# Moving an adaptive-modulation weight stream towards the gate projections, and the sums of h into the first up-projection group

## The chip, the cores and the metric

The kernel runs on one core of a Trainium2 chip. The metric is the device time of one execution in microseconds (us). The engines named below are PE (TensorE, the matrix engine), DVE (VectorE), ACT (ScalarE), POOL (GpSimd) and SP (SyncE, which here only issues DMAs). Each works through its own queue in order. A tile of 128 partitions by 512 columns of float32 is 256 KB.

## What is computed

One layer of a hybrid decoder on 512 tokens of width 2048, in float32. A vector c gives six modulation rows; two mixers and a feed-forward part with a causal convolution of width 3 follow:

```python
mod = (silu(c) @ w_ada + b_ada)[:, None, :]
sh_a, sc_a, gt_a, sh_f, sc_f, gt_f = jnp.split(mod, 6, axis=-1)
h = rms_norm(x, g_attn) * (1.0 + sc_a) + sh_a
# h @ w_in gives, among others, the columns gate_a and gate_b (2048 each)
merged = sigmoid(gate_a) * (o_a @ w_pa) + sigmoid(gate_b) * (o_b @ w_pb)
x = x + gt_a * (merged @ w_o)
h = rms_norm(x, g_ffn) * (1.0 + sc_f) + sh_f
u = conv3_causal(h @ w_up)
x = x + gt_f * ((silu(u[..., :5632]) * u[..., 5632:]) @ w_down)
```

Here o_a is a sparse attention (8 heads, keys chosen by an indexer) and o_b a dense latent attention (8 heads).

## The kernel before, in words

**Arithmetic.** Each float32 operand is split into a rounded part hi and a rest lo (`split`: ACT makes hi, L116, DVE makes lo, L117), and a product is three matmuls, hi x hi, hi x lo and lo x hi (`mm3`, L120 to L122). Weights pass through `wtile`: SP loads a pair of 128-row blocks, 512 KB, into a raw tile (L105), ACT and DVE split it (L109, L110) into one of three hi/lo pairs. These instructions get a high priority.

**Order.** The framework arranges the instructions of each engine at build time, from a simulated timeline, with the place in the program as priority. A later part can so fill the gaps of an earlier one, but the order on the chip is fixed. Data dependences go by the program: who writes a tile waits for all who used it before in the program.

**Storage.** There are 75 slots of 128 x 512 (`get` takes the one that has been free longest, `put` gives it back), eight PSUM banks, and five raw tiles, used strictly in turn by the weights and by the ada stream (`raw_tile`). In the middle of the kernel banks 0 to 3 (`MM`) serve projections; banks 4 to 7 (`AT`) serve the attention and are handed out in turn by `at_bank()`.

**Stages**, with their place in the profiled span: the first four modulation rows' part and the indexer's projections (to 230 us), the indexer and the query projection (to 350), attention A interleaved with the gate projections (to 550), the rest of the gates (to 667), the latent projections MKV and MQ (`C_MKV`, `C_MQ`), attention B interleaved with the projection by w_pa, the projection by w_pb (to about 1160), the output projection by w_o (to 1355), the second norm that makes h2, up group 0 (to 1455), then 40 pairs of column blocks of the up projection by a scheme of seven products in place of eight (L1258 to L1260), and the down projection.

The gate projections are eight blocks (`gate_block`). Blocks 0 to 5 stand right after attention A in the program, block 6 after the latent projections. A block calls `lin_fm`, which runs over the 16 row blocks two at a time: 8 ticks of 24 matmuls (block 7 has 2 ticks). `pa_block` and the loop over w_pb have 4 ticks for each of four column blocks; the output projection has 8 ticks for each of four. After each tick a function `tick` may be called.

**The ada stream.** 16 column blocks of w_ada are not needed until later (gt_a, sc_f, sh_f, gt_f). `ada_stream` is a generator: each call of `next` loads 512 KB into a raw tile (L715) and adds it on DVE to an accumulator (two operations, L720 for the first of a block and L722). Eight calls make a block; the ninth puts the finished block on the list `pend` and begins the next. There are two accumulators, used alternately. `ticker(rate)` adds `rate` to a credit at each tick and calls `next` for every whole unit: TG holds the rates of the gate blocks, TP that of w_pa, TB of w_pb, TO of w_o. What is left over runs after w_o.

`flush_cols(b)` finishes the blocks of `pend`: it splits the accumulator into two new slots, sums over the partitions with two matmuls into bank b (L749, L750), and then either loads b_ada into the accumulator by a DMA on POOL, adds the bank (L754) and stores the result to DRAM (L755, eight of the blocks), or picks the diagonal into `mod` (L758 and the lines behind it). Before, it is called at the start of each block of the gates, of w_pa, w_pb and w_o, with the fourth bank of those that the block will use.

**The sums of h.** The seven-product scheme needs four sums of quarters of h2, `tsum`. They are formed from `x1T`, 16 tiles that hold the normed and scaled x: four steps, each with 8 DVE operations on half tiles (L1123 to L1126) and 4 splits. They stand behind up group 0 in the program. `up_group(0)` runs `lin_fm` twice (gate and value columns, 16 ticks in all), with the convolution (`conv`) at the end of each.

Of the kernel before, what the change touches and what calls it, by code (L numbers as in the profile page):

```python
# [14 lines left out]
AF = mybir.ActivationFunctionType  # L15
ALU = mybir.AluOpType
AX = mybir.AxisListType

P = 128
T = 512  # L20
D = 2048
KD = D // P
# [4 lines left out]
C_MQ, C_MKV, C_GA, C_GB = 2640, 3152, 3472, 5520  # L27
# [4 lines left out]
def trunk_layer_kernel(  # L32
# [9 lines left out]
    U1=4,  # L42
    U2=10,
    PLAN="A0 A1|A2 A3|B0 B1 B2 B3|A4 A5 A6 A7|B4 B5 B6 B7|A8 A9 A10 A11|B8 B9 B10 B11|A12 A13 A14 A15 B12 B13 B14 B15",
    TG=(0, 1, 1, 1, 1, 1, 1, 1),
    TP=1.5,
    TB=1.5,
    TO=1,
    HG=2,
    AFT=(-1,),  # L50
    PEU=((2, 5, 8, 11, 14),) * 2 + ((),) * 6,
# [2 lines left out]
    V, A, G, PE, SP = nc.vector, nc.scalar, nc.gpsimd, nc.tensor, nc.sync  # L54
# [18 lines left out]
    def getr():  # L73
        return get(F32R)

    def put(*ts):
        for t in ts:
            free.append(held.pop(id(t)))
# [45 lines left out]
    def lin_fm(src, c0, act, K, banks, evac, tick=None, M=4):  # L124
        kn = 8 // M
        for kg in range(0, K, kn):
            wh, wl = wtile(src, kg, kn, c0, M * P)
            for m in range(M):
                ms = slice(m * P, (m + 1) * P)
                for i in range(kn):  # L130
                    k = kg + i
                    ah, al = act[k]
                    mm3(banks[m], wh[:, i, ms], wl[:, i, ms], ah, al, k == 0, k == K - 1)
                if kg + kn == K:
                    evac(m, banks[m])
            if tick:
                tick()
# [16 lines left out]
    def half():  # L154
        cnt["half"] += 1
        return bank[4:8] if cnt["half"] % 2 == 0 else bank[0:4]
# [94 lines left out]
    for ks in (range(0, 7), range(7, 14), range(14, KD)):  # L251
# [4 lines left out]
        for k in ks:  # L256
            t = get()
# [16 lines left out]
    h = []  # L274
# [95 lines left out]
    for g in range(-2, 8):  # L370
# [7 lines left out]
        if 0 <= g + 1 < 8:  # L378
            ada_cols(g + 1)
            for k in (2 * g + 2, 2 * g + 3):  # L380
                hi, lo, t = getr(), getr(), ht[k % 2]
# [108 lines left out]
    MM = bank[0:4]  # L490
# [10 lines left out]
    b = bank[7]  # L501
# [10 lines left out]
    b = bank[6]  # L512
# [7 lines left out]
    for tb in range(1, 4):  # L520
        S = (tb + 1) * P
        qiT = []
        for cb in range(2):
            t = qi[tb, cb]
            rope(t.rearrange("p (h d) -> p h d", d=64), 8, 16, "i", tb)
            b = at_bank()
# [8 lines left out]
        for hd in range(16):  # L535
            ps = slice((hd % 2) * 64, (hd % 2) * 64 + 64)
            q = (hd % 8) // 2
            b = at_bank()
# [20 lines left out]
        gt, eq, pre = rl[1][:, :S], rl[2][:, :S], wk[:, :S]  # L559
# [30 lines left out]
    for tb in range(4):  # L590
        t = kva[tb]
# [8 lines left out]
    for g in range(2):  # L600
        b = at_bank()
# [105 lines left out]
    ada_acc = [get(), get()]  # L707
# [20 lines left out]
    pend = []  # L728
# [2 lines left out]

    credit = [0.0]

    def ticker(rate):
        def tick():
            credit[0] += rate
            while credit[0] >= 1.0:
                credit[0] -= 1.0
                next(stream, None)
        return tick  # L740

# [2 lines left out]
    def flush_cols(b):  # L744
        while pend:
            cb, acc = pend.pop(0)
            hi, lo = getr(), getr()
            split(hi, lo, acc)
            PE.matmul(b, ones_r, hi, start=True, stop=False)  # L749
            PE.matmul(b, ones_r, lo, start=False, stop=True)  # L750
            put(hi, lo)
            if cb in gtr_d:
                G.dma_start(acc, b_ada[0:1, cb * 512:(cb + 1) * 512].to_broadcast([P, T]))
                V.tensor_tensor(acc, acc, b, ALU.add)  # L754
                G.dma_start(gtr_d[cb], acc)  # L755
            else:
                a3 = acc.rearrange("p (q n) -> p q n", q=4)
                V.tensor_tensor(a3, b.rearrange("p (q n) -> p q n", q=4),  # L758
                                ident[:, None, :].to_broadcast([P, 4, P]), ALU.mult)
                s4 = sm.tile([P, 4], F32, name="ss4")  # L760
                V.tensor_reduce(s4, a3, axis=AX.X, op=ALU.add)
                mod_cols(mod[:, cb * 4:cb * 4 + 4], s4, col1[:, cb * 4:cb * 4 + 4])
# [11 lines left out]
    gate_d = [dram.tile([P, T], F32, name=f"gate{k}") for k in range(2 * KD)]  # L774
# [4 lines left out]
    def ev_store(dst, j0):  # L779
        def ev(m, b):  # L780
            t = gst[m % 2]
            if m % 2:
                V.tensor_copy(t, b)
            else:
                A.activation(t, b, AF.Copy)
            G.dma_start(dst[j0 + m], t)
        return ev

    def gate_block(n):
        flush_cols(MM[3])  # L790
        j0 = 3 + n * 4
        lin_fm(w_in, C_GA + j0 * P, h, KD, MM, ev_store(gate_d, j0), tick=ticker(TG[n]), M=1 if n == 7 else 4)

    for n in range(GA1):
        gate_block(n)
# [148 lines left out]
    def pa_block(cb):  # L944
        flush_cols(MM[3])
        lin_fm(w_pa, cb * 512, oa, 8, MM, ev_store(pa_d, cb * 4), tick=ticker(TP))

# [54 lines left out]
    for cb in range(4):  # L1002
        bk = half()
        flush_cols(bk[3])
        lin_fm(w_pb, cb * 512, ob, 8, bk, ev_pb(load_gates(cb)), tick=ticker(TB))
    for t in ob:
# [37 lines left out]
    for db in range(4):  # L1044
        bk = half()
# [13 lines left out]
    bk = half()  # L1059
# [5 lines left out]
    h2 = []  # L1065
    lo_i = []
    for k in range(KD):
        t = x1T[k]
# [10 lines left out]
    def conv(j, b):  # L1079
        t = get()  # L1080
        A.activation(t, b, AF.Identity, bias=wcv[:, 3, j:j + 1], scale=wcv[:, 2, j:j + 1])
        V.scalar_tensor_tensor(t[:, 1:], b[:, :T - 1], wcv[:, 1, j:j + 1], t[:, 1:], op0=ALU.mult, op1=ALU.add)
        V.scalar_tensor_tensor(t[:, 2:], b[:, :T - 2], wcv[:, 0, j:j + 1], t[:, 2:], op0=ALU.mult, op1=ALU.add)
        return t
# [2 lines left out]
    NG = DFF // 512  # L1087
    f_d = [dram.tile([P, T], F32, name=f"f{j}") for j in range(NF_)]

    def up_group(grp):  # L1090
        gt = []

        def ev_g(m, b):
            t = conv(grp * 4 + m, b)
            A.activation(t, t, AF.Silu)
            gt.append(t)

        bk = half()
        flush_cols(bk[3])
        lin_fm(w_up, grp * 512, h2, KD, bk, ev_g)  # L1100

        def ev_v(m, b):
            t = conv(44 + grp * 4 + m, b)
            V.tensor_tensor(t, t, gt[m], ALU.mult)
            G.dma_start(f_d[grp * 4 + m], t)
            put(t, gt[m])

        lin_fm(w_up, 512 + grp * 512, h2, KD, half(), ev_v)

    up_group(0)  # L1110
    put(*ada_acc)


    HT = T // 2
    KH = KD // 2
    tsum = [[], [], [], []]
    for i in range(KH // 2):
        raw = [get() for _ in range(4)]
        for j in range(2):
            k, o = 2 * i + j, slice(j * HT, (j + 1) * HT)  # L1120
            ta, tb_ = x1T[k], x1T[k + KH]
            b1, b2 = mod[:, 48 + k:49 + k], mod[:, 48 + k + KH:49 + k + KH]
            V.tensor_tensor(raw[0][:, o], ta[:, HT:], ta[:, :HT], ALU.subtract)  # L1123
            V.scalar_tensor_tensor(raw[1][:, o], tb_[:, HT:], b2, raw[0][:, o], op0=ALU.add, op1=ALU.subtract)
            V.scalar_tensor_tensor(raw[2][:, o], ta[:, :HT], b1, raw[1][:, o], op0=ALU.add, op1=ALU.subtract)
            V.scalar_tensor_tensor(raw[3][:, o], tb_[:, :HT], b2, raw[1][:, o], op0=ALU.add, op1=ALU.subtract)  # L1126
            put(ta, tb_)
        for n in range(4):
            hi, lo = getr(), getr()
            split(hi, lo, raw[n])  # L1130
            tsum[n].append((hi, lo))
        put(*raw)

    def quarter(k0, c0):
        return [(h2[k0 + k][0][:, c0:c0 + HT], h2[k0 + k][1][:, c0:c0 + HT]) for k in range(KH)]
# [131 lines left out]
    for j in range(NF_):  # L1267
        t = get()
# [63 lines left out]
```

## Time and profile before

| | us |
|---|---|
| median of 3 runs | 2770.88 |
| lowest, highest | 2768.09, 2776.09 |
| the profiled execution | 2772.84 |
| its span | 2771.1 |

Page lines and views are read so. In the groups, a row names the line, engine and operation, the written and the read tiles, the count, the busy time, the mean of one in ns, and then the idle time of the engine before these instructions with what ended it. In a window row stand the start and end, the length, then for PE, PEld (weight loads), DVE, ACT and POOL the busy time with the number of instructions (x), then the granted clock of TensorE as a share, the mean share of the DMA engines and GB/s; where a row is for one line alone, only the engines that it uses are listed. A wait row names who waited for whom, the total, the times and the longest. A timeline row has the start, the duration, engine, line and operation, and in brackets the idle time before it and what ended it.

### The profile page before, as it was taken

How to read it: one execution, taken by the hardware profiler on the slowest of the kernel's cores; microseconds unless marked ns; L12 is line 12 of the kernel's file. 1: busy time of each engine (PE TensorE's matmuls, PEld its weight loads, DVE VectorE, ACT ScalarE, POOL GpSimd, SP SyncE). 2: the span in 40 equal slices, each digit the busy share in tenths (PEclk: the TensorE clock that was granted, in tenths of full speed). 3: DMA queues.
4: the chain of work that ended last, by engine and by line, in shares of the span. 5: the costliest groups of instructions: out<-in, count | busy, mean ns of one | idle time of the engine just before them, and what ended most of it. 6: DMA issues, size and time to landing. Idle time of an engine off the chain costs nothing.

```text
span 2771.1 us, 38675 instructions
## 1 busy us (share of the span) xinstructions
PE 2684.6 (97%) x15040; PEld 2293.4 (83%) x15040; DVE 1858.2 (67%) x2931; ACT 1110.5 (40%) x1637; POOL 225.3 (8%) x443
## 2 busy tenths in 40 slices
PE   6999999999999999998998999999999999999998
PEld 5877777788886767776788999999999997888887
DVE  6987975544467676745658888888888873325333
ACT  4333433322344555222434555555555553223221
POOL 1000010100122232100000000000000030000000
PEclk8999999999999999999999999999999999999999
DMA  9943245565475397765422333333333373243232
GB/s 322 356 141 96 60 138 165 183 215 173 125 233 163 128 314 235 267 201 184 139 84 99 119 121 120 118 123 117 121 118 120 121 276 131 91 129 122 94 104 84
DMA packets 197931, 432.93 MB, mean 156 GB/s; under 512 B 18122, under 2 KB 59492, under 8 KB 197748
## 3 DMA queue, kind: packets, MB, share of 16 engines
q1 hardware_dynamic: 168884, 348.59, 39.2%
q0 software_dynamic: 28832, 81.88, 8.6%
q8 instruction: 117, 1.92, 0.3%
q14 instruction: 66, 0.54, 0.1%
q10 hardware_dynamic: 32, 0.01, 0.0%
HBM read 388.46 MB, written 41.94 MB: 155 GB/s over the span
## 4 chain that ended last, share of the span: by engine, by line
PE 74%; issue 13%; DMA 6%; DVE 4%; POOL 1%; ACT 1%; SPq 0%; POOLq 0%; DVEq 0%; ACTq 0%
PE bank L120 14%; PE bank L121 14%; PE bank L122 14%; PE bank L1259 10%; PE bank L1258 10%; PE bank L1260 10%; DMA raw<-in_w_ada 3%; DMA slot<-in_w_ada 1%; DVE wlo L110 1%; DVE slot L722 1%; PE bank L676 1%; DMA raw<-in_w_in 1%; PE bank L931 1%; DMA slot<-in_x 0%; DMA slot<-gate 0%
## 5 line engine op out<-in xcount | busy, mean ns | idle before, releaser
L109 ACT ACTIVATE whi<-raw 128x1024 fp32r<-128x1024 f32 (+4 forms) x302 | 314.3, 1042 | 828.9 <-PE bank L122 506.2
L1259 PE MATMUL bank<-slot,whi 128*128 128x256 f32 x2240 | 628.5, 281 | 7.0 <-DVE slot L117 7.0
L1258 PE MATMUL bank<-slot,whi 128*128 128x256 f32 x2240 | 628.3, 281 | 5.0 <-ACT slot L116 3.2
L1260 PE MATMUL bank<-slot,wlo 128*128 128x256 f32 x2240 | 624.2, 281 | 0.0
L120 PE MATMUL bank<-whi,slot 128*128 128x512 f32 (+2 forms) x1472 | 575.0, 395 | 24.1 <-DVE slot L754 9.9
L121 PE MATMUL bank<-wlo,slot 128*128 128x512 f32 (+2 forms) x1472 | 579.3, 394 | 4.8 <-DVE wlo L110 4.5
L122 PE MATMUL bank<-whi,slot 128*128 128x512 f32 (+2 forms) x1472 | 566.9, 391 | 0.0
L110 DVE TENSOR_TENSOR wlo<-raw,whi 128x1024 fp32r<-128x1024 f32 (+4 forms) x302 | 362.9, 1203 | 301.2 <-ACT whi L109 298.2
L116 ACT ACTIVATE whi<-raw 128x1024 fp32r<-128x1024 f32 x280 | 297.4, 1062 | 339.9 <-PE bank L1259 248.7
L1258 PEld LDWEIGHTS bank<-slot,whi 128*128 128x128 f32 x2240 | 424.1, 189 | 5.9 <-ACT slot L116 3.5
L1259 PEld LDWEIGHTS bank<-slot,whi 128*128 128x128 f32 x2240 | 422.5, 189 | 7.2 <-DVE slot L117 7.2
L1260 PEld LDWEIGHTS bank<-slot,wlo 128*128 128x128 f32 x2240 | 419.9, 189 | 0.0
L117 DVE TENSOR_TENSOR wlo<-raw,whi 128x1024 fp32r<-128x1024 f32 x280 | 341.7, 1221 | 67.6 <-ACT whi L116 65.3
L120 PE MATMUL bank<-slot,whi 128*128 128x512 f32 (+1 forms) x912 | 361.0, 401 | 3.4 <-ACT slot L1072 1.4
L121 PE MATMUL bank<-slot,whi 128*128 128x512 f32 (+1 forms) x912 | 363.5, 399 | 0.1
L122 PE MATMUL bank<-slot,wlo 128*128 128x512 f32 (+1 forms) x912 | 357.5, 399 | 0.0
L120 PEld LDWEIGHTS bank<-whi,slot 128*128 128x128 f32 x1472 | 280.0, 190 | 91.5 <-DVE slot L754 11.4
L121 PEld LDWEIGHTS bank<-wlo,slot 128*128 128x128 f32 x1472 | 280.4, 190 | 67.5 <-DVE wlo L110 7.7
L122 PEld LDWEIGHTS bank<-whi,slot 128*128 128x128 f32 x1472 | 278.7, 189 | 61.2 <-issue 0.9
L722 DVE SCALAR_TENSOR_TENSOR slot<-raw,c_act,slot 128x512 f32<-128x512 f32 x240 | 179.7, 749 | 126.5 <-DMA raw<-in_w_ada 123.6
L117 DVE TENSOR_TENSOR slot<-slot,slot 128x512 fp32r<-128x512 f32 x136 | 92.2, 692 | 194.6 <-PE bank L121 188.7
L120 PEld LDWEIGHTS bank<-slot,whi 128*128 128x128 f32 (+1 forms) x912 | 170.7, 187 | 43.8 <-ACT whi L109 2.1
(279 smaller groups left out, 2619.9 us busy)
## 6 DMA issues: line engine op xcount, KB each, us to landing
raw<-in_w_ups SPq DMA_DIRECT2D x160, 512.0 KB, 3.5
raw<-in_w_ada SPq DMA_DIRECT2D x128, 512.0 KB, 4.9
raw<-in_w_down SPq DMA_DIRECT2D x88, 512.0 KB, 3.6
raw<-in_w_in SPq DMA_DIRECT2D x82, 512.0 KB, 3.7
slot<-in_w_ada SPq DMA_DIRECT2D x128, 256.0 KB, 6.0
raw<-in_w_o SPq DMA_DIRECT2D x32, 512.0 KB, 4.8
f<-slot POOLq DMA_DIRECT2D x44, 256.0 KB, 2.4
slot<-f POOLq DMA_DIRECT2D x44, 256.0 KB, 6.5
```

The lines of the kernel that those rows point to most:

```text
L109: A.activation(hi, raw[:, :w], AF.Copy)
L110: V.tensor_tensor(lo, raw[:, :w], r32(hi), ALU.subtract)
L116: A.activation(dst_hi, src, AF.Copy)
L117: V.tensor_tensor(dst_lo, src, r32(dst_hi), ALU.subtract)
L120: PE.matmul(o, lh, rh, start=first, stop=False)
L121: PE.matmul(o, lh, rl, start=False, stop=False)
L122: PE.matmul(o, ll, rh, start=False, stop=last)
L676: PE.matmul(ob[:, kc * P:], vf(kc), pt[3 - kc], start=kc == 0, stop=kc == 3)
L722: V.scalar_tensor_tensor(acc, t[:, i], c_act[:, k:k + 1], acc, op0=ALU.mult, op1=ALU.add)
L1258: PE.matmul(o, wh[:, ks], rh, start=first and k == 0, stop=False, skip_group_check=True)
L1259: PE.matmul(o, wh[:, ks], rl, start=False, stop=False, skip_group_check=True)
L1260: PE.matmul(o, wl[:, ks], rh, start=False, stop=last, skip_group_check=True)
```

## The change

The rates of the ada stream change: gate blocks from (0, 1, 1, 1, 1, 1, 1, 1) to (1, 1.5, 1.5, 1.5, 1.5, 1.5, 1.5, 1), w_pa and w_pb from 1.5 to 1, w_o from 1 to 0.5. In the gate blocks `flush_cols` is no longer called at the start with the fourth projection bank; instead `tick` calls it, when a finished block is on `pend`, before the next call of the stream, with a bank from `at_bank()`. The four steps of the sums become a function, called after ticks 2, 4, 6 and 10 of up group 0; each of the raw tiles of a step is put back as soon as it is split, and the two ada accumulators are put back ahead of up group 0 rather than behind it.

```diff
-    TG=(0, 1, 1, 1, 1, 1, 1, 1),
-    TP=1.5,
-    TB=1.5,
-    TO=1,
+    TG=(1, 1.5, 1.5, 1.5, 1.5, 1.5, 1.5, 1),
+    TP=1,
+    TB=1,
+    TO=0.5,
...
-    def ticker(rate):
+    def ticker(rate, fb=None):
         def tick():
             credit[0] += rate
             while credit[0] >= 1.0:
                 credit[0] -= 1.0
+                if fb and pend:
+                    flush_cols(fb())
                 next(stream, None)
         return tick
...
     def gate_block(n):
-        flush_cols(MM[3])
         j0 = 3 + n * 4
-        lin_fm(w_in, C_GA + j0 * P, h, KD, MM, ev_store(gate_d, j0), tick=ticker(TG[n]), M=1 if n == 7 else 4)
+        lin_fm(w_in, C_GA + j0 * P, h, KD, MM, ev_store(gate_d, j0), tick=ticker(TG[n], at_bank), M=1 if n == 7 else 4)
...
-    up_group(0)
-    put(*ada_acc)
...
     tsum = [[], [], [], []]
-    for i in range(KH // 2):
+
+    def sum_step(i):
         raw = [get() for _ in range(4)]
...
             tsum[n].append((hi, lo))
-        put(*raw)
+            put(raw[n])
+
+    steps_done = [0]
+
+    def sum_tick():
+        steps_done[0] += 1
+        if steps_done[0] in (2, 4, 6, 10):
+            sum_step(len(tsum[0]))
+
+    def up_group(grp):
...
-        lin_fm(w_up, grp * 512, h2, KD, bk, ev_g)
+        lin_fm(w_up, grp * 512, h2, KD, bk, ev_g, tick=sum_tick)
...
-        lin_fm(w_up, 512 + grp * 512, h2, KD, half(), ev_v)
+        lin_fm(w_up, 512 + grp * 512, h2, KD, half(), ev_v, tick=sum_tick)
+
+    put(*ada_acc)
+    up_group(0)
```

More of the change, by code (lines that the diff above doesn't have):

```diff
@@ L1088, in trunk_layer_kernel @@
     f_d = [dram.tile([P, T], F32, name=f"f{j}") for j in range(NF_)]
[L1090 to L1099, printed above, removed]
-        lin_fm(w_up, grp * 512, h2, KD, bk, ev_g)
[L1102 to L1106, printed above, removed]
-        lin_fm(w_up, 512 + grp * 512, h2, KD, half(), ev_v)
-    up_group(0)
-    put(*ada_acc)
     HT = T // 2
@@ L1131, in trunk_layer_kernel, with ev_g, ev_v @@
             tsum[n].append((hi, lo))
-        put(*raw)
+            put(raw[n])
[5 more added lines that the diff above has]
+    def up_group(grp):
+        gt = []
+        def ev_g(m, b):
+            t = conv(grp * 4 + m, b)
+            A.activation(t, t, AF.Silu)
+            gt.append(t)
+        bk = half()
+        flush_cols(bk[3])
+        lin_fm(w_up, grp * 512, h2, KD, bk, ev_g, tick=sum_tick)
+        def ev_v(m, b):
+            t = conv(44 + grp * 4 + m, b)
+            V.tensor_tensor(t, t, gt[m], ALU.mult)
+            G.dma_start(f_d[grp * 4 + m], t)
+            put(t, gt[m])
+        lin_fm(w_up, 512 + grp * 512, h2, KD, half(), ev_v, tick=sum_tick)
+    put(*ada_acc)
+    up_group(0)
     def quarter(k0, c0):
```

## The prediction

> **What bounds the kernel now.** I read the busy table of the page first, then the span in windows of 50 and 10 us for stretches where TensorE (PE) loses matmuls, then in those the waits and the timeline.
>
> ```profile
> span 2771.1 us, 38675 instructions
> PE 2684.6 (97%) x15040; PEld 2293.4 (83%) x15040; DVE 1858.2 (67%) x2931; ACT 1110.5 (40%) x1637; POOL 225.3 (8%) x443
> ```
>
> PE has work nearly always, so only stalls of PE can be gained. The busy column hides them; the number of matmuls in a window (x) shows them.
>
> ```profile
> 1150.00:1200.00 50.00, 47.66 (x202) 37.34 (x200) 33.11 (x46) 11.28 (x13) 3.22 (x6) 1.00 0.71 231
> 1200.00:1250.00 50.00, 45.57 (x183) 35.92 (x183) 24.65 (x33) 11.56 (x17) 3.25 (x6) 0.93 0.55 180
> 1250.00:1300.00 50.00, 45.30 (x188) 36.02 (x187) 25.21 (x33) 11.57 (x17) 3.24 (x6) 0.97 0.60 199
> 1300.00:1350.00 50.00, 44.54 (x176) 34.82 (x176) 22.90 (x29) 11.79 (x17) 3.24 (x6) 0.93 0.54 179
> ...
> 2300.00:2350.00 50.00, 50.00 (x217) 40.40 (x216) 17.27 (x18) 14.02 (x18) 0.00 (x0) 1.00 0.29 95
> ```
>
> The last row is a full window: 217 matmuls of 512 columns, 50/217 = 0.230 us each, so one tick (24 matmuls, one pair of weight rows) is 5.53 us. In the output projection (1200 to 1350) 34 + 29 + 41 = 104 matmuls are missing: 24.0 us.
>
> ```profile
> DVE slot L722 <- DMA raw<-in_w_ada: 72.6, 22, 6.2
> ...
> PE bank L120 <- DVE slot L754: 9.9, 3, 4.2
> ...
> PE bank L121 <- DVE wlo L110: 4.5, 3, 2.2
> ```
> ```profile
> 1313.19 0.75 DVE L722 SCALAR_TENSOR_TENSOR slot<-raw,c_act,slot 128x512 f32<-128x512 f32 x1 [2.27 <-DMA raw<-in_w_ada]
> 1313.86 0.68 DVE L1028 TENSOR_TENSOR slot<-slot,slot 128x512 f32<-128x512 f32 x1
> 1314.46 0.68 DVE L754 TENSOR_TENSOR slot<-slot,bank 128x512 f32<-128x512 f32 x1
> 1315.06 0.68 DVE L1028 TENSOR_TENSOR slot<-slot,slot 128x512 f32<-128x512 f32 x1
> 1315.66 1.22 DVE L110 TENSOR_TENSOR wlo<-raw,whi 128x1024 fp32r<-128x1024 f32 x1
> ```
>
> The reason is VectorE's (DVE) order: an ada step (L722) waits there for its DMA, 72.6 us in this stage, and behind it stand the flush that must empty the fourth bank (L754) and the weight split (L110). PE waits for both.
>
> The second loss lies where up group 0 ends and the seven-product scheme begins:
>
> ```profile
> 1450.00:1460.00 10.00, 8.92 (x54) 7.73 (x52) 9.25 (x13) 6.77 (x9) 1.13 (x2) 1.00 0.29 107
> 1460.00:1470.00 10.00, 1.44 (x5) 1.14 (x5) 10.00 (x20) 3.20 (x6) 1.08 (x2) 0.60 0.30 105
> 1470.00:1480.00 10.00, 7.64 (x45) 7.15 (x46) 5.76 (x10) 4.85 (x9) 0.00 (x0) 0.72 0.00 1
> 1480.00:1490.00 10.00, 10.00 (x87) 10.00 (x86) 9.04 (x11) 4.01 (x4) 0.00 (x0) 1.00 0.33 107
> ```
> ```profile
> PE bank L1259 <- DVE slot L117: 7.0, 1, 7.0
> PE bank L1258 <- ACT slot L116: 3.2, 1, 3.2
> ```
> ```profile
> 1402.47 0.89 DVE L1125 SCALAR_TENSOR_TENSOR slot<-slot,mod,slot 128x256 f32<-128x256 f32 x2
> ...
> 1459.02 0.68 DVE L117 TENSOR_TENSOR slot<-slot,slot 128x512 fp32r<-128x512 f32 x1
> ...
> 1469.98 4.31 DVE L117 TENSOR_TENSOR slot<-slot,slot 128x512 fp32r<-128x512 f32 x7
> ```
>
> With 87 as full, 82 + 42 = 124 matmuls of 256 columns are missing, 14.2 us. The sums of h are half done by 1403, then stand until 1459: their next slots are those that the convolution of up group 0 gives back at its end.
>
> **The change part by part.**
>
> *Sums.* Nothing is removed and no DMA is in it; L1123 to L1126 and 16 splits are issued inside up group 0. Asked for earlier, they get slots that are long free: at its start 32 of h2 and 16 of x1T are held of 75, so 27 are free once the two accumulators are put back; step 0 takes 12 and returns 8, as do the others. The work after 1459 (12 of the 16 splits at 0.6 us, and some 5 us of L1123 to L1126, 12 us together) moves before 1450.
>
> ```profile
> 1420.00:1430.00 10.00, 10.00 (x44) 8.06 (x43) 2.45 (x2) 2.12 (x2) 0.00 (x0) 1.00 0.17 54
> 1430.00:1440.00 10.00, 10.00 (x44) 8.09 (x44) 1.76 (x2) 2.12 (x2) 0.00 (x0) 1.00 0.33 105
> ```
>
> DVE has over 15 us idle in these two rows alone, so the work costs nothing there; without that cover it would cost its 12 us. What is late next is the last convolution, already in the 1450 row; I leave 2 us. Gain 14.2 - 2 = 12 us (9 to 14).
>
> *Output projection.* TO falls from 1 to 0.5: 16 ada steps instead of some 30, one per 11 us. Their loop (split L110 frees the raw tile, the DMA lands, L722, the next L110) takes about 0.1 + 5 + 1.4 + 1.2 = 7.7 us, over the 5.53 us of a tick and under two ticks. So the waits go; flushes remain at two block starts, at 2 to 3 us each. Of 24 us, 18 are gained (10 to 22).
>
> *Branch projections.* TP and TB fall from 1.5 to 1. The stall there:
>
> ```profile
> 1030.00:1040.00 10.00, 6.43 (x21) 3.20 (x20) 8.30 (x19) 7.27 (x10) 2.48 (x5) 0.94 1.08 401
> 1040.00:1050.00 10.00, 8.01 (x23) 4.78 (x23) 2.32 (x9) 9.03 (x16) 2.15 (x4) 0.55 0.60 210
> ```
>
> DMA is full in the first row; fewer ada steps leave it room. But attention, ACT and reloads are in it too. I take 4 us with the fewer flushes in the main banks (0 to 8).
>
> *Gates.* TG puts 82 calls of the stream into the gate blocks instead of 50: 8 in block 0, 12 in blocks 1 to 6, 2 in block 7. Each is one DMA and two DVE operations:
>
> ```profile
> L722 DVE SCALAR_TENSOR_TENSOR slot<-raw,c_act,slot 128x512 f32<-128x512 f32 x240 | 179.7, 749 | 126.5 <-DMA raw<-in_w_ada 123.6
> ...
> raw<-in_w_ada SPq DMA_DIRECT2D x128, 512.0 KB, 4.9
> ```
>
> The added wait is in the flush. It now takes an attention bank, and in the program all of attention A stands ahead of it: 137th use, the bank that head 7 used for its second group of transposes. So the first flush (call 10) waits for the end of attention A, and the third ada block (call 17) waits for its accumulator. Behind it stand, on DVE the L722 of all later calls, on SP their DMAs (no raw tile comes free), on POOL the flush's load and store among the gate stores; the order in a queue is fixed when the program is built, so weights whose DMA stands behind such an ada DMA wait too. At rate 1.5 the five tiles are used in two ticks, so the weights keep two tiles of their own and go on, until the latent projections use all five.
>
> ```profile
> 500.00:530.00 30.00, 0.00 (x0) 1.00 0.48 156
> 530.00:560.00 30.00, 11.25 (x15) 1.00 0.75 239
> ...
> 587.00:604.00 17.00, 10.16 (x14) 1.00 0.81 250
> 604.00:633.00 29.00, 1.10 (x2) 1.00 0.58 198
> 633.00:651.00 18.00, 9.76 (x13) 1.00 0.76 246
> ```
> ```profile
> 540.00:550.00 10.00, 0.87 (x5) 0.64 (x5) 1.00 0.86 274
> 550.00:560.00 10.00, 0.00 (x0) 0.00 (x0) 1.00 0.95 309
> ```
> ```profile
> 531.75 0.69 DVE L754 TENSOR_TENSOR slot<-slot,bank 128x512 f32<-128x512 f32 x1 [2.99 <-PE bank L750]
> ...
> 535.45 0.49 DVE L720 TENSOR_SCALAR slot<-raw,c_act 128x512 f32<-128x512 f32 x1 [1.20 <-DMA gtr<-slot]
> ```
> ```profile
> 669.01 0.54 POOL L786 DMA_DIRECT2D gate<-slot  x1 [0.46 <-DVE slot L783]
> ```
>
> The first five rows (L722 alone, two operations a step, the first of a block being L720) show this wait in the kernel before: no step from 500 to 530, then bursts of 8 steps, each held until the next block's flush. The transposes (L668, next rows) end near 548; from L754 to the next L720 are 3.7 us, so call 17 starts near 553. Block 5 ends with its store at 669; the second weight tile of the latent projection needs call 66 some 7 us before its use, by 662. These are 50 calls in 109 us, three of them loaded: 47 x r + 3 x 1.5 us, where r = 2.22 us just fits. The bursts give 17/8 = 2.1 and 18/8 = 2.3 us with three to five tiles loaded beforehand; I take 2.6 without that: 127 us, and PE stands for 127 - 109 = 18 us; 2 less for the flushes that no longer wait for a gate bank: 16 us. Ends, counted likewise: 2 (r = 2.3) and 35 (r = 3). Until 550 the same 16 calls run as before: 0 (-4 to +6).
>
> [...]
>
> [...]
>
> *Sum.* -12 - 18 - 4 + 16 = -18 us on the profiled execution's 2772.8 us: 2754.8. That run lay 2.0 us above the median of 2770.9, so 2753 us.
>
> **The rivals.**
>
> *The stream catches up in time.* If the bursts' 2.1 to 2.3 us hold, the stall is 0 to 4 us, say 2: about 2770.9 - 34 + 2 = 2739. For it: DVE was at 10.2 of 17 us with L722 in a burst and PE lost little there. Against: those bursts began with loaded tiles.
>
> *The gates become the bound (slower).* The stream stands until attention A ends, and its backlog holds the latent projections. If the three ada tiles give only r = 3.75 us, as the weakest row did (530 to 560: 8 steps in 30 us), the stall is 47 x 3.75 + 4.5 - 109 = 72 us, and the time 2770.9 + 72 - 34 = 2809. It decides from a stall of 34 us on, r = 2.94 us. For it: the bursts end after 8 steps, so no row shows a longer run at under 3 us. Against: 250 GB/s in the bursts left room.
>
> *The change doesn't do what it says in the output projection.* If the step that is left still stands ahead of the evacuation at block starts, the 18 us shrink to 5: 2766. For it: three of the stalls are at block starts, and loads and stores of x meet there. Against: half the steps, and a loop shorter than two ticks.
>
> **How the numbers follow.** Forecast 0.50 (2753, itself 2741 to 2767), catch-up in time 0.20 (2739), gates bound 0.17 (2772 to 2809), output projection unmoved 0.13 (2766). The range 2732 to 2778 leaves out the upper part of the third and a tail below. Some 0.3% (8 us) is what a measurement can tell from no change: under 2762.6 is faster, over 2779.2 slower. Faster: 0.20 + 0.46 = 0.66; slower: 0.14, from the third; the rest, 0.20, is the same.
>
> **What would show it.** Right: 87 matmuls in every 10 us window of the 30 us after up group 0; over 205 matmuls in each 50 us window of the output projection; no L722 between call 16 and the end of attention A, then a run of 50 calls with DMA over 300 GB/s; a PE stall near the first latent projection, with SP waiting there for L722. Wrong: the first flush done before head 7's transposes (no backlog), a stall over 34 us, or DVE still waiting over 40 us for ada DMAs in the output projection.

## The result, and the profile after

The changed kernel takes 2732.15 us (median of 4 runs, 2731.34 to 2732.21), the kernel before beside it 2773.49 us (4 runs, 2768.09 to 2778.7): a ratio of 0.985, with 0.9829 to 0.9872 as its 95% interval. Some 41 us were gained where 18 were forecast. The profiled execution took 2732.16 us. First the busy table of its page:

```profile
span 2730.4 us, 38657 instructions
...
PE 2668.3 (98%) x15040; PEld 2284.3 (84%) x15040; DVE 1855.8 (68%) x2931; ACT 1112.2 (41%) x1639; POOL 229.0 (8%) x443
```

As before, the busy column tells little; the windows tell where matmuls are missing. The next fence has the changed kernel's windows, all engines: the output projection, the end of up group 0, and the end of the gates.

```profile
1150.00:1200.00 50.00, 50.00 (x217) 40.42 (x216) 27.27 (x36) 12.34 (x17) 5.93 (x11) 1.00 0.60 199
1200.00:1250.00 50.00, 50.00 (x217) 40.41 (x216) 21.72 (x27) 12.95 (x19) 3.24 (x6) 1.00 0.54 172
1250.00:1300.00 50.00, 50.00 (x217) 40.44 (x216) 21.81 (x26) 12.87 (x18) 2.70 (x5) 1.00 0.55 172
...
1420.00:1430.00 10.00, 10.00 (x49) 8.21 (x48) 8.37 (x11) 4.44 (x6) 0.60 (x1) 1.00 0.18 54
1430.00:1440.00 10.00, 10.00 (x87) 10.00 (x86) 9.40 (x11) 4.68 (x8) 1.62 (x3) 1.00 0.40 147
1440.00:1450.00 10.00, 10.00 (x86) 10.00 (x86) 9.18 (x11) 4.94 (x6) 0.00 (x0) 1.00 0.40 121
...
660.00:670.00 10.00, 4.01 (x18) 3.34 (x18) 8.15 (x14) 0.60 (x1) 1.17 (x3) 0.72 0.82 263
670.00:680.00 10.00, 3.21 (x8) 1.79 (x7) 8.84 (x15) 0.63 (x1) 0.43 (x1) 0.50 0.85 265
680.00:690.00 10.00, 7.34 (x33) 7.34 (x34) 3.60 (x7) 2.21 (x3) 0.00 (x0) 0.59 0.62 184
690.00:700.00 10.00, 10.00 (x70) 10.00 (x69) 2.26 (x3) 1.95 (x3) 0.00 (x0) 1.00 0.47 134
```

The output projection has 217 matmuls in each row, the full number, where it had 202, 183 and 188. The seven-product scheme now starts at full speed: 87 and 86 matmuls in the rows behind 1430, no row of 5. The new loss is in the three rows from 660 to 690, where the latent projections begin. They hold 18 + 8 + 33 = 59 matmuls where three rows like that from 690 hold 210: 151 are missing, 21.6 us. PE was idle for 30 - 14.6 = 15.4 us of them; the rest is matmuls at a granted clock of 0.50 to 0.72.

To put numbers on the stretches I counted in the traces when a certain matmul starts: the 1100th, 1700th, 2300th and 3900th of the 7152 that read a split weight outside the seven-product scheme, and then the first matmul of the second norm, the first and last of the scheme, and the last of all. Their order on PE is the program's, so the times between two of them compare like with like, except that the end of attention A can move between the second and the third stretch. In us:

| stretch | before | after | difference | forecast |
|---|---|---|---|---|
| to the 1100th (gates begin) | 358.1 | 353.4 | -4.7 | 0 |
| to the 1700th (end of attention A) | 186.0 | 179.5 | -6.5 | 0 |
| to the 2300th (gates end, latent projections) | 136.6 | 162.3 | +25.7 | +16 |
| to the 3900th (attention B, w_pa, w_pb) | 469.1 | 456.9 | -12.2 | -4 |
| to the second norm (w_o) | 204.4 | 176.0 | -28.4 | -18 |
| up group 0 | 100.9 | 100.8 | -0.1 | 0 |
| seven-product scheme | 809.8 | 794.5 | -15.3 | -12 |
| the rest | 497.1 | 497.9 | +0.8 | 0 |
| last matmul starts | 2762.0 | 2721.3 | -40.7 | -18 |

The stall went as foretold. The windows of the ada steps' line in the changed kernel (busy time and count of L722 on DVE, then the clock, the DMA share and GB/s):

```profile
400.00:410.00 10.00, 4.49 (x6) 1.00 0.91 296
410.00:420.00 10.00, 0.00 (x0) 1.00 0.57 186
...
530.00:540.00 10.00, 0.00 (x0) 1.00 0.44 140
540.00:550.00 10.00, 1.41 (x2) 1.00 0.25 80
...
560.00:570.00 10.00, 5.24 (x7) 1.00 1.01 353
...
670.00:680.00 10.00, 6.78 (x10) 0.50 0.85 265
```

No step between 410 and 540, then a run without a pause. How fast it is stands in the group of the DMA's line, for 540 to 690 (the count, the issue's ns, the first and last start):

```profile
L715 SPq DMA_DIRECT2D raw<-in_w_ada x49: 367/368/512, 549.3 to 676.1; - x49
```

49 loads from 549.3 to 676.1 are 126.8/48 = 2.64 us a step; the prediction had taken r = 2.6 and a start near 553. A load takes 5.3 us from issue to landing there in the median, so the last one lands near 681; PE resumes at 682.7. Who kept PE waiting from 650 to 700 (total, times, longest):

```profile
PE bank L120 <- ACT whi L109: 6.4, 1, 6.4
PE bank L120 <- DVE slot L785: 6.0, 2, 3.2
PE bank L751 <- ACT slot L116: 2.5, 1, 2.5
```

SP's own waits from 540 to 700 show what holds the loads:

```profile
SPq L715 <- DVE slot L722: 67.6, 48, 6.5
```

Two things stand behind the backlog: the next weights (the split, L109, waits for a raw tile) and the emptying of the last gate block's banks (L785 here is L783 of the kernel before), which DVE does in order behind L722. The forecast named the first only. The stretch to the 2300th matmul grew by 25.7 us, 4 more than the stall: 636 matmuls lie in it against 616.

### The profile page after: what moved, and what is told of

Its sections match the earlier page's. It is cut to its first block, busy times and chain, and to the rows that moved or that the text cites. A ratio compares the mean times of both kernels' runs of the same rounds, so it can differ in the third digit from the quotient of the medians.

```text
span 2730.4 us, 38657 instructions
## 1 busy us (share of the span) xinstructions
PE 2668.3 (98%) x15040; PEld 2284.3 (84%) x15040; DVE 1855.8 (68%) x2931; ACT 1112.2 (41%) x1639; POOL 229.0 (8%) x443
## 4 chain that ended last, share of the span: by engine, by line
PE 88%; issue 5%; DMA 4%; DVE 2%; ACT 1%; POOL 1%; SPq 0%; DVEq 0%; POOLq 0%; ACTq 0%
PE bank L120 18%; PE bank L121 18%; PE bank L122 18%; PE bank L1268 9%; PE bank L1267 9%; PE bank L1269 9%; DMA slot<-in_w_ada 1%; PE bank L676 1%; PE bank L932 1%; PE bank L692 1%; PE bank L668 1%; DMA slot<-gate 0%; DMA slot<-in_x 0%; DMA raw<-in_w_down 0%; PE bank L933 0%
## 5 line engine op out<-in xcount | busy, mean ns | idle before, releaser
L109 ACT ACTIVATE whi<-raw 128x1024 fp32r<-128x1024 f32 (+4 forms) x302 | 314.3, 1042 | 823.5 <-PE bank L122 538.2
L722 DVE SCALAR_TENSOR_TENSOR slot<-raw,c_act,slot 128x512 f32<-128x512 f32 x240 | 179.2, 747 | 112.5 <-DMA raw<-in_w_ada 109.6
L122 PEld LDWEIGHTS bank<-slot,wlo 128*128 128x128 f32 (+1 forms) x912 | 171.3, 188 | 42.3 <-DVE wlo L110 1.9
```

The source lines that it names most:

```text
L109: A.activation(hi, raw[:, :w], AF.Copy)
L122: PE.matmul(o, ll, rh, start=False, stop=last)
L722: V.scalar_tensor_tensor(acc, t[:, i], c_act[:, k:k + 1], acc, op0=ALU.mult, op1=ALU.add)
```

## The experiments

All of these kernels compute the same layer. "Ahead at the end of attention A" means: the start of the last score matmul (L692) compared with the kernel before, plus 0.23 us for each weight matmul done more by then (0.230 us is the full rate), less what the run was ahead at the first matmul of L302. That line sums the first modulation rows, which the first normalised column block waits for; it starts near 34 or 38 us, and the expectations give these times to the column block.

**One half each.** First the sums alone, with the rates, the ticker and the gate blocks of the kernel before; then the stream alone, with the sums behind up group 0.

```diff
-    TG=(1, 1.5, 1.5, 1.5, 1.5, 1.5, 1.5, 1),
-    TP=1,
-    TB=1,
-    TO=0.5,
+    TG=(0, 1, 1, 1, 1, 1, 1, 1),
+    TP=1.5,
+    TB=1.5,
+    TO=1,
...
     def gate_block(n):
+        flush_cols(MM[3])
```

> Only the sums of h are moved; rates and flushes as before. Local theory: the 15 us that PE loses around 1450 to 1480 in the kernel before vanish, nothing else moves: about 2758 us (ratio 0.9945). Rival (the moved sums only crowd DVE in up group 0, the gain of the whole change comes from the stream): 2765 to 2775 us, with new PE losses between 1360 and 1450.

```diff
-        lin_fm(w_up, grp * 512, h2, KD, bk, ev_g, tick=sum_tick)
+        lin_fm(w_up, grp * 512, h2, KD, bk, ev_g)
...
-    put(*ada_acc)
     up_group(0)
+    put(*ada_acc)
...
+    for i in range(KH // 2):
+        raw = [get() for _ in range(4)]
```

> Only the stream is moved; the sums stay behind up group 0. Local theory: the rest of the gain, 41 - 15 = 26 us, so about 2747 us, with the loss of 15 us in the first windows of the seven-product scheme still there and a PE stall of some 22 us at the first latent projection. Rival (the two parts only pay together): under 10 us gained, 2763 us or more.

The sums alone: 2756.73 us, ratio 0.9937 (0.9915 to 0.996). The seven-product stretch took 793.0 us there, 16.8 less, and nothing else moved by over 3 us. The stream alone: 2752.77 us, ratio 0.9919 (0.9899 to 0.9939). The two parts are independent and add up: some 17 to 20 and 21 to 24 us (against 2773.49 and 2776.25, the medians of the kernel before in the two sets of runs).

**The output projection.** w_o back at one step a tick, w_pa and w_pb at 0.5 so that the number of steps fits; then the same with each finished block flushed after a tick, into a bank that the block does not use.

```diff
-    TP=1,
-    TB=1,
-    TO=0.5,
+    TP=0.5,
+    TB=0.5,
+    TO=1,
```

> As the changed kernel, but the stream's calls that stand in the branch and output projections are divided as TP 0.5, TB 0.5, TO 1, so that the output projection has the rate of before with the gates unchanged. Theory (DVE waits in its order for ada DMAs in the output projection): the loss there comes back, 20 to 28 us, about 2755 us, with over 50 us of DVE waits for ada DMAs in that stage. Rival (the loss there came from what reaches the stage from the branch projections at rate 1.5): it stays away, within 5 us of the changed kernel, 2732 to 2737 us.

```diff
-        lin_tm(w_o, db * 512, 512, mg, KD, bk, ev_o(db), tick=ticker(TO))
+        lin_tm(w_o, db * 512, 512, mg, KD, bk, ev_o(db), tick=ticker(TO, lambda b=bk: (bank[0:4] if b[0] is bank[4] else bank[4:8])[3]))
```

> The run with w_pa and w_pb at 0.5 and w_o at 1, and besides each finished block is flushed in w_o after a tick, into the fourth bank of the half that the block does not use, in place of at the next block's start. Theory (PE waits in w_o because DVE waits for ada transfers in order, wherever the flush is): PE still loses 25 us or more between 1100 and 1400, 2748 to 2758 us. Rival (the flush at the block start, ahead of the evacuation, is what PE pays): under 15 us are lost there, 2735 to 2742 us.

2753.65 us, ratio 0.9927 (0.9907 to 0.9948), and 2756.47 us in one run. The windows of the second:

```profile
1200.00:1250.00 50.00, 44.77 (x184) 35.17 (x183) 22.93 (x30) 11.36 (x17) 3.26 (x6) 0.97 0.57 193
1250.00:1300.00 50.00, 44.07 (x185) 34.53 (x186) 25.54 (x33) 11.45 (x17) 3.25 (x6) 1.00 0.56 183
```

33 and 32 matmuls of 217 are missing again, 15 us in 100, though no flush stands at a block's start. The stretch of w_o takes 208.3 and 208.7 us in the two kernels against 176.0. The flush is not what PE pays there, the step's rate is. The row of DVE's waits for ada loads from 1100 to 1330 in the second kernel, and then in the changed one:

```profile
DVE slot L722 <- DMA raw<-in_w_ada: 100.7, 26, 9.9
```

```profile
DVE slot L722 <- DMA raw<-in_w_ada: 57.0, 12, 7.1
```

DVE still waits 57 us for ada loads in the changed kernel, 5 us at a time, and PE loses nothing (72.6 us and 22 times in the same stretch before). The prediction had named more than 40 us of it as a sign that it was wrong; that sign was badly chosen. I take it that what counts is how often the wait comes: with a step in every second tick, one tick's weights can be split late and the next makes it good. That is argued; these runs change the number of the waits and their sum together.

**The backlog.** Four kernels ask how it reaches PE. One moves steps out of gate blocks 4 and 5 into the latent projections; one gives the weights raw tiles 0 and 1 and the stream tiles 2 to 4; one takes gate rate 1; one starts the stream a block later.

```diff
-    TG=(1, 1.5, 1.5, 1.5, 1.5, 1.5, 1.5, 1),
+    TG=(1, 1.5, 1.5, 1.5, 1, 0.5, 1.5, 1),
...
-    TB=1,
-    TO=0.5,
+    TB=0.75,
+    TO=0.375,
+    TL=(1, 1.5),
...
-    lin_tm(w_in, C_MKV, 320, h, KD, MM, ev_mkv)
+    lin_tm(w_in, C_MKV, 320, h, KD, MM, ev_mkv, tick=ticker(TL[0], at_bank))
-    lin_tm(w_in, C_MQ, 512, h, KD, MM, ev_mq)
+    lin_tm(w_in, C_MQ, 512, h, KD, MM, ev_mq, tick=ticker(TL[1], at_bank))
```

> As the changed kernel, but 20 calls of the stream stand in the latent projections (rates 1 and 1.5 there), gate blocks 4 and 5 have rates 1 and 0.5, w_pb 0.75 and w_o 0.375. Theory (the stall of 22 us is a backlog: some 52 calls between the end of attention A and the latent projections at 2.6 us each, behind which the raw tiles of the weights stand): 40 calls fit, the stall falls under 5 us, about 2714 us. Rival (the latent projections start late whatever the backlog, by the evacuation of the last gate block or by their own loads): over 15 us of the stall stay, 2725 us or more.

2758.87 us, ratio 0.9945 (0.9925 to 0.9965): a miss, and worse than the change. Its windows, all engines:

```profile
580.00:590.00 10.00, 2.71 (x12) 1.86 (x10) 6.27 (x10) 0.00 (x0) 0.54 (x1) 0.74 0.85 289
590.00:600.00 10.00, 1.59 (x2) 0.58 (x2) 7.31 (x11) 0.63 (x1) 0.54 (x1) 0.50 0.85 280
600.00:610.00 10.00, 0.00 (x0) 0.00 (x0) 7.79 (x11) 0.55 (x1) 0.54 (x1) 0.50 0.82 257
610.00:620.00 10.00, 1.59 (x2) 0.57 (x2) 8.79 (x14) 0.08 (x1) 0.00 (x0) 0.50 0.78 244
```

and PE's waits from 580 to 630 (its lines lie one further down than in the changed kernel):

```profile
PE bank L752 <- ACT slot L117: 25.2, 2, 15.0
PE bank L121 <- ACT whi L110: 11.2, 1, 11.2
```

The stall came some 80 us sooner and was larger: 16 matmuls in 40 us. PE stood 25.2 us at the sums of a flush, waiting for the finished ada block, and 11.2 for weights. I had counted steps and forgotten the tiles. At rate 1.5 five tiles are used in exactly two ticks, so the weights always get the same two; where the rate drops to 1, the weights move on to tiles that the stream's backlog holds. That this is the reason is argued here: the next two kernels test the turn of the tiles, and none takes apart the larger wait, that at the flush.

```diff
+        if two_rings[0]:
+            key, first, n = ("rawa", 2, 3) if ada else ("raww", 0, 2)
```

> From the gates to the end of the output projection the weights use raw tiles 0 and 1 in turn, the ada stream tiles 2 to 4; nothing else differs from the changed kernel. Theory (the backlog reaches PE because weights stand behind ada transfers in the strict turn of five raw tiles): the stall of 22 us at 650 to 700 falls under 6 us, the rest stays, about 2712 us (2706 to 2720). Rival (the backlog reaches PE over DVE's and POOL's order, or over the DMA rate, not over the raw tiles): over 12 us of it stay, 2722 us or more. A second way to miss: two tiles are too few for the weights where transfers take long (w_pa, 1000 to 1100), and 5 to 10 us are lost there.

2714.59 us, ratio 0.9787 (0.9764 to 0.981). Its window at the end of the gates:

```profile
650.00:700.00 50.00, 44.80 (x258) 40.26 (x257) 41.08 (x61) 11.60 (x19) 2.15 (x4) 1.00 0.91 304
```

The stretch to the 2300th matmul takes 143.2 us in place of 162.3: 19 of the 25.7 us are gone, 6.6 remain, a little over the 6 of the theory. So most of the stall was the shared turn of the raw tiles. The remainder was not taken apart.

```diff
-    TG=(1, 1.5, 1.5, 1.5, 1.5, 1.5, 1.5, 1),
+    TG=(1, 1, 1, 1, 1, 1, 1.5, 1),
-    TP=1,
-    TB=1,
-    TO=0.5,
+    TP=1.5,
+    TB=1.5,
+    TO=0.625,
```

> Gate rates 1 in blocks 0 to 5 and 1.5 in block 6, w_pa and w_pb at 1.5, w_o at 0.625: the stream has about the pace of the kernel before in the gates, but with the flush in the attention banks. Theory (at rate 1 the five tiles are used in 2.5 ticks, so weights and ada share every tile and the weights stop when the stream waits for the end of attention A): PE loses 30 to 60 us between 400 and 550, 2745 to 2780 us. Rival (the weights go on at any rate, and fewer calls in the gates mean a smaller backlog): loss in 350 to 550 under 15 us, stall at 650 to 700 under 8 us, about 2722 us.

2760.82 us in one run, as the theory had it, with a smaller loss in the gates than it said: PE is idle for 12.5 us from 350 to 550, and the stretch from the 1100th to the 1700th matmul is 25 us longer than in the changed kernel. Its window 500 to 550 has 170 matmuls where the changed kernel has 226:

```profile
500.00:550.00 50.00, 43.02 (x170) 33.04 (x169) 32.09 (x46) 12.44 (x16) 6.50 (x12) 0.90 0.81 266
```

Attention A ended 37 us sooner there, at 500.3, with 1512 weight matmuls done in place of 1717: the weights starved, and attention, which needs none, ran ahead.

```diff
-    TG=(1, 1.5, 1.5, 1.5, 1.5, 1.5, 1.5, 1),
+    TG=(0, 1.5, 1.5, 1.5, 1.5, 1.5, 1.5, 1),
...
-    TB=1,
+    TB=1.5,
```

> Rate 0 in gate block 0 in place of 1, w_pb at 1.5 in place of 1; the rest as in the changed kernel. Theory (the 10 us gained at 350 to 550 come from the stream standing still from 410 to the end of attention A, so that its DMAs and DVE work do not meet attention's gathers): with 8 calls fewer the stream goes on longer before it stands, losses at 350 to 550 rise from 13 to 17 to 23 us, while the backlog shrinks by 8 steps only if the stand begins at the same call; stall at 650 to 700 between 12 and 22 us; 2728 to 2742 us. Rival (the gain at 350 to 550 has nothing to do with the stream): losses there stay within 2 us of 13 and the time is 2722 to 2732 us.

2713.07 us, ratio 0.978 (0.9754 to 0.9806): faster than either expectation. The window at the end of the gates, then the DMA group from 530 to 660:

```profile
650.00:700.00 50.00, 50.00 (x290) 45.84 (x289) 21.17 (x50) 14.37 (x34) 4.38 (x8) 1.00 0.55 166
```

```profile
L715 SPq DMA_DIRECT2D raw<-in_w_ada x41: 367/368/377, 539.1 to 647.2; - x41
```

Eight loads fewer, at 108.1/40 = 2.70 us each: the last is issued at 647.2, and nothing stalls (136.6 us to the 2300th matmul, as before the change). Here the prediction's own sum was better than what I expected of this run: with 39 steps it is 39 x 2.6 + 4.5 = 106 us, under the 109 that it had.

**Beside attention B.** As many steps in all, but more of them in w_pa:

```diff
-    TP=1,
-    TB=1,
+    TP=1.5,
+    TB=0.5,
```

> w_pa at 1.5 in place of 1 and w_pb at 0.5 in place of 1, as many calls in all. Theory (the gain of 11 us at 800 to 1100 comes from the thinner stream beside attention B and w_pa): the losses at 800 to 1100 rise by 6 to 11 us, 2738 to 2743 us. Rival (that gain comes from the flushes' new places and banks): they stay within 3 us, 2729 to 2735 us.

2738.44 us in one run. The time is that of the theory, its reason is not: the stretch from the 2300th to the 3900th matmul takes 458.2 us there against 456.9, and 5.3 of the 6 us are already missing at the start of L302 (39.1 against 33.8), which nothing in this kernel touches. The rival stands: the 12 us do not come from taking the stream from 1.5 to 1 in w_pa.

A thinner stream can still pay there. The two kernels with 0.5 in both w_pa and w_pb, built for the output projection, take 448.2 and 447.6 us for this stretch, 9 less than the changed kernel at 1, whose stall near 1030 is gone in them. The window in the changed kernel, then in the first of the two:

```profile
1000.00:1050.00 50.00, 47.27 (x175) 31.28 (x174) 24.93 (x58) 25.76 (x42) 18.86 (x36) 0.93 0.86 273
```

```profile
1000.00:1050.00 50.00, 50.00 (x205) 33.89 (x203) 27.35 (x60) 34.80 (x55) 17.90 (x34) 1.00 0.80 263
```

They lost more than that in the output projection, where the steps went.

**Beside attention A.** The first 16 steps spread over attention A:

```diff
-    TG=(1, 1.5, 1.5, 1.5, 1.5, 1.5, 1.5, 1),
+    TG=(1, 0.5, 0.5, 1, 1.5, 1.5, 1.5, 1),
-    TP=1,
-    TB=1,
-    TO=0.5,
+    TP=1.5,
+    TB=1.5,
+    TO=0.625,
```

> The gates' rates are 1, 0.5, 0.5, 1, then 1.5 in three blocks and 1; w_pa and w_pb 1.5, w_o 0.625. The first 16 calls of the stream so spread over attention A instead of ending at 410 and standing. Theory (attention A runs with less loss when the stream stands): the 5 to 6 us by which the changed kernel is ahead at the end of attention A, counted in weight matmuls done, shrink to 2 or less; no stall over 5 us at 650 to 700, since fewer calls pile up; w_pa and w_pb lose some 10 us again; 2720 to 2732 us. Rival (the gain beside attention A comes from the flush in the attention banks and not from the standing stream): it stays at 5 to 6 us.

2741.05 us. Attention A ended at 535.9 with 1704 weight matmuls done, against 537.3 and 1672: 1.4 + 32 x 0.23 - 3.6 = 5.2 us ahead, as in the changed kernel (537.5 and 1717: -0.2 + 10.4 - 4.1 = 6.1). The theory of the standing stream falls. The time missed its range (2720 to 2732): w_o at 0.625 takes 190.0 us, 14 more than at 0.5. So I crossed the rates with the place of the flush: the new flush with the old rates, and the old flush (block start, fourth projection bank) at gate rate 1, to be set beside the run at rate 1 above.

```diff
-    TG=(1, 1.5, 1.5, 1.5, 1.5, 1.5, 1.5, 1),
+    TG=(1, 1, 1, 1, 1, 1, 1, 1),
-    TP=1,
-    TB=1,
-    TO=0.5,
+    TP=1.5,
+    TB=1.5,
+    TO=0.75,
...
     def gate_block(n):
+        flush_cols(MM[3])
         j0 = 3 + n * 4
-        lin_fm(w_in, C_GA + j0 * P, h, KD, MM, ev_store(gate_d, j0), tick=ticker(TG[n], at_bank), M=1 if n == 7 else 4)
+        lin_fm(w_in, C_GA + j0 * P, h, KD, MM, ev_store(gate_d, j0), tick=ticker(TG[n]), M=1 if n == 7 else 4)
```

> Gates at rate 1 in all eight blocks with the flush as in the kernel before (at each block's start, in the fourth projection bank), w_pa and w_pb 1.5, w_o 0.75; the sums as in the changed kernel. To be set beside the run at gate rate 1 with the flush in the attention banks (2760.8 us). Theory (there the weights starved because the flush's attention bank comes free only at the end of attention A): the weights do not starve, attention A ends near 537 us as before and not at 500, no loss over 5 us in any 50 us between 550 and 700, 2738 to 2750 us. Rival (the flush waits for slots that attention A holds, not for the bank): attention A ends near 500 again, 2755 us or more.

```diff
-    TG=(1, 1.5, 1.5, 1.5, 1.5, 1.5, 1.5, 1),
-    TP=1,
-    TB=1,
-    TO=0.5,
+    TG=(0, 1, 1, 1, 1, 1, 1, 1),
+    TP=1.5,
+    TB=1.5,
+    TO=1,
```

> The rates of the kernel before with the flush of the changed one (in the gates after a tick, in an attention bank); the sums as in the changed kernel. Theory (the 5 to 6 us by which the changed kernel is ahead at the end of attention A come from the flushes' new place): they stay, and since at rate 1 weights and ada steps share all five tiles, 10 to 20 us are lost in the gates while the stream stands; w_o loses its 28 us; 2755 to 2775 us. Rival (they come from the rates): attention A is ahead by 1 us or less, once its end is put at the same number of weight matmuls.

The new flush with the old rates: 2741.33 us in one run, 14 below the lower end of what was expected: the stream stood only from 489.5 to 534.5 us, and the weights hardly starved. Attention A ended at 529.0 with 1672 done, 8.3 - 3.7 = 4.6 us ahead. The old flush at rate 1: 2751.38 us, ended at 535.5 with 1686, 1.8 + 3.2 - 4.2 = 0.8 us ahead; the sums alone, also with the old flush, at 537.1 with 1672, 0.2 + 0.7 = 0.9 (its L302 began at 38.6, not at 37.9). So the 5 us go with the flush's form, at all the rates tried at which the weights do not starve; with the new flush at rate 1, where they starve, the same sum is 37.0 - 36.8 - 3.6 = -3.4 us.

They also show where a part of the branch gain is. PE's waits from 870 to 900 with the old flush and old rates (the sums-only kernel), first rows:

```profile
PE bank L875 <- DVE slot L865: 1.6, 2, 1.1
PE bank L879 <- DVE slot L671: 1.1, 1, 1.1
```

The windows 860 to 910 of the kernel before, then of the changed one:

```profile
860.00:910.00 50.00, 46.45 (x204) 34.30 (x203) 35.28 (x107) 21.65 (x49) 10.32 (x16) 0.93 0.55 173
```

```profile
860.00:910.00 50.00, 50.00 (x228) 37.21 (x228) 35.11 (x110) 22.91 (x53) 9.99 (x13) 1.00 0.41 132
```

All three kernels with the old flush (before, the sums alone, the old flush at rate 1) have PE idle for 2.7 to 3.9 us between 880 and 900. The granted clock of the kernel before was 0.66 from 880 to 890 (0.93 in the whole first row), that of the changed one 1.00. In the changed kernel, in the one with two rings (50.00 of 50 us busy from 860 to 910 in both) and with the new flush at the old rates (no wait of PE from 870 to 900) PE is not idle there. The stretch from the 2300th to the 3900th matmul took 469.1, 471.7 and 473.1 us with the old flush, and 455.0, 459.7 and 464.3 with the new one at the same rates of 1.5 in w_pa and w_pb. The stream at 1 (456.9) adds nothing to that, and the three values of the new flush lie 9 us apart, one run each. What of the flush does it was not separated: its bank, its slots, or that each flush takes a place in the turn of `at_bank()` and so moves all later uses.

The old flush at rate 1 also moved the stand: the steps stop from 422 to 468, eight calls run, and they stop again from 489 to 550, where the changed kernel has one stand from 408 to 548. But the weights starved there too, which the theory had denied, and the time lies just over its range:

```profile
500.00:550.00 50.00, 43.20 (x171) 30.87 (x170) 19.09 (x53) 14.37 (x34) 8.20 (x15) 0.91 0.33 103
```

So the attention bank accounts for the first eight calls of the stand (16 to 24), and something else that attention A holds, most likely the slots, for the rest; that part is argued, not shown.

**Two more.** The changed kernel once more, and the run without steps in gate block 0 with 20 steps moved from the branches into the latent projections (with the ticks that the first of the backlog's kernels has there):

> The changed kernel once more, unaltered. Theory (the 4 us by which its profiled execution was ahead at 34 us, before any changed instruction, are a matter of the single execution): the first normalised column block begins near 38 us in the profile, and the span is 2 to 5 us longer, 2732 to 2737 us. Rival (they belong to the built program): again near 34 us, 2731 to 2733 us.

```diff
-    TG=(1, 1.5, 1.5, 1.5, 1.5, 1.5, 1.5, 1),
-    TP=1,
-    TB=1,
+    TG=(0, 1.5, 1.5, 1.5, 1.5, 1.5, 1.5, 1),
+    TP=0.5,
+    TB=0.75,
+    TL=(1, 1.5),
```

> As the run without ada steps in gate block 0 (2713 us), and besides the two latent projections take the stream at 1 and 1.5 calls a tick (20 calls), w_pa falls to 0.5 and w_pb to 0.75. Theory (the backlog is worked off by 655, DMA is under half busy from 660 to 750, and fewer steps in the branches cost less there): no stall at 650 to 700, 0 to 8 us less between 750 and 1100, 2705 to 2713 us. Rival (20 steps make the latent projections wait, or what is lost in the branches no longer comes from the ada steps): 2714 us or more.

The changed kernel again took 2733.86 us, and its L302 began at 34.4 us, near the 33.8 of the first time and unlike 37.9 in the kernel before. The latent steps gave 2713.61 us, ratio 0.9786 (0.977 to 0.9803): no gain over 2713.07 that these runs can tell. The stretch from the 2300th to the 3900th matmul takes 452.1 us there against 452.0, with the 20 calls in it; what the thinner branches gained and what the latent steps cost was not separated. The three best kernels lie within 1.6 us of each other, some 18 us under the change as made.

## Why the prediction was off

The sum of the parts was 22.7 us short: -18 was forecast, and by the table -40.7 came. The output projection gave 10.4 us more than its term, the part until 550 gave 11.2, the branch projections 8.2 and the sums 3.3; the stretch of the stall took 9.7 more than its term, and the rest 0.7.

- **The chain of the backlog was right**: the stand from call 16 to the end of attention A (row 410 to row 540), the run at 2.64 us a step (2.6 forecast), the stall at the first latent projection, and SP held by L722. The stretch grew by 25.7 us where 16 were forecast (the stall itself is 21.6), in the main because the deadline was taken from the profile before. PE reached the latent projection at 659.7 instead of 667.2, while the stream's last load is fixed by the end of attention A (537.5 against 537.3). What is gained ahead of such a stall is paid back in it: to the 2300th matmul the sum of three stretches is +14.5 us, and the forecast was +16. Matmuls at a granted clock of 0.50 to 0.72 took some 6 of the 21.6, beside the 15.4 us in which PE was idle.
- **The sums** were right in place and cause, and short in size: "I leave 2 us" for the last convolution was not needed. 15.3 us in place of 12; alone 16.8.
- **The output projection is the step that failed most**, the largest error among the terms of the sum that were priced: "Of 24 us, 18 are gained", since "flushes remain at two block starts, at 2 to 3 us each". They cost nothing (217 matmuls in each row of 50 us), and the rows 1200 to 1350 were not the whole stage: the row from 1150, quoted in the prediction, lacks 217 - 202 = 15 matmuls, 3.5 us more. 24.0 + 3.5 = 27.5 was there to be gained, and 28.4 came. The runs at one step a tick, with the flush in either place, lose it again. So the step's rate was the right cause and the size was wrong; "the waits go" holds for PE alone, since DVE still waits 57 us there.
- **The branch projections**: "fewer ada steps leave it room" is not what gave the 12.2 us, and 4 us was the wrong size. At unchanged rates the new flush alone gives 14 in one run (455.0 against 469.1), and going from 1.5 to 1 adds nothing; only the step from 1 to 0.5, which this change does not make, gave room worth 9 us.
- **The flush in the gates** was priced as a wait, with "2 less" for the banks. Its form is worth some 10 us by itself, as far as one run tells. The new flush with the old rates, set beside the sums alone, starts its last matmul 15.2 us sooner (2730.4 against 2745.6), and 5.0 of these lie before the 1100th matmul, where nothing was changed. Then the new rates give 9.1 us net (2721.3): 25.0 gained in w_o, 21.7 lost in the stall, and 5.8 gained in small pieces elsewhere.
- **Until 550** the prediction put nothing: "the same 16 calls run as before: 0 (-4 to +6)". 11.2 us came. The 4.7 us to the 1100th matmul belong to no step: PE's order there is the same in both kernels. The 6.5 us in attention A go with the flush's form; by what way stays open.

The rivals: the catch-up in time (2739) was nearest in time and wrong in cause, since r was 2.64 and not 2.3. Gates bound and an unmoved output projection did not come. The range's lower end of 2732 held the time by 0.15 us, which is luck; it left out that several small terms could all fall short on the same side.

## What to carry to other kernels

A stream that waits for one late event and then catches up has a finish time that does not move with the engine it feeds: count its steps from the event, and take some of them away before it rather than speed up what stands ahead of the stall; with eight steps fewer this kernel took 19 us less. Where two streams share one ring of buffers, work out which of them gets which buffer at each rate, for a rate that lowers the load can put the critical one behind the stuck one; a ring for each costs nothing here and removed most of the stall. When a flush or an evacuation changes its buffers, price what leaves the old place as well as the wait in the new one.

## What was not expected of the hardware

Between 12 and 38 us, with the same instructions in the same order, the kernel before and the changed one differ by 4 us. The group of PE's first transposes (ns: least, median, most), before and after:

```profile
L254 PE MATMUL bank<-ident,slot x64: 272/421/477, 12.5 to 34.5; 128*128 128x128 f32 x64
```

```profile
L254 PE MATMUL bank<-ident,slot x64: 272/276/477, 12.5 to 30.1; 128*128 128x128 f32 x64
```

More of them ran slowly in the first. Of the 16 profiles, ten began L302 at 33.7 to 34.4 us, and the other six at 37.9 to 39.1. The windows from 20 to 30, before and after, show a granted clock of 1.00 for both:

```profile
20.00:30.00 10.00, 10.00 (x49) 9.77 (x48) 8.39 (x18) 2.06 (x4) 0.00 (x0) 1.00 1.08 366
```

```profile
20.00:30.00 10.00, 10.00 (x82) 9.77 (x81) 9.93 (x21) 4.65 (x9) 0.00 (x0) 1.00 1.08 366
```

So the profile's record of the clock does not show a cause. Whether the 4 us belong to the built program or to the single execution, the two profiles of the changed kernel (33.8 and 34.4) do not decide; they may as well have been alike by chance. The cause of these 4 us stays open.

While the backlog ran, DMA moved 326 GB/s over 50 us, and up to 353 in 10 us, with PE at full speed beside it. Two windows of the changed kernel, all engines:

```profile
560.00:570.00 10.00, 10.00 (x45) 8.12 (x44) 8.47 (x11) 3.05 (x4) 1.63 (x3) 1.00 1.01 353
...
600.00:650.00 50.00, 50.00 (x217) 40.46 (x216) 43.45 (x60) 11.35 (x13) 2.69 (x5) 1.00 0.94 326
```

DMA's mean busy share was 1.01 and 0.94 in these two rows, so the 2.64 us a step may be near what DMA gives with weights and stores beside the stream; that is an estimate. But DMA moved more elsewhere, 401 GB/s in the row at 1030 before and 366 in the rows from 20 to 30, and DVE was busy for 43.45 of the 50 us in the second row; which of the two set the pace is not shown, and no run had a faster DVE.
